# Two transformer-like blocks on one core: the order in which dense matmuls of 512 columns walk through their columns

## The chip, the core and the metric

The kernel runs on one core of one Trainium2 chip. The metric is the device time of one execution in microseconds, lower is better; a kernel is given by the median of several executions. A profile is one further execution, recorded by the hardware profiler; its span reaches from the first to the last instruction.

## The reference

One sequence of 1024 tokens of width 1024, with 16 learned tokens in front, goes through two blocks in float32. What matters here is where the dense products are:

```python
# first block
proj  = h @ w_in                       # then three mixers: HGRN2, Mamba2, S5
mixed = concatenate([y_a, y_b, y_c]) @ w_out
h  = layer_norm(ALPHA * h + mixed)
ff = square(relu(h @ w_mlp_in)) @ w_mlp_out     # 1024 -> 4096 -> 1024
h  = layer_norm(ALPHA * h + ff)
# second block: a gated delta rule and a spatial gating branch, each with its own
# projections, a gated sum, an output projection, and a feed-forward part of width 2 x 2816
```

The mixers are sequences of small products and elementwise work on chunks of tokens; the projections and the feed-forward parts are large products with K, M and N of hundreds to thousands.

## The kernel before

All tokens are processed in two halves of 512 tokens (the first with the 16 learned ones in front). Dense products keep float32 accuracy by three products of a rounded format: `split` and `weights` make of each operand a high part (ScalarE copies it to the format `F32R`, tiles `xt` and `wh`) and a low part (VectorE subtracts, tiles `xt` and `wl`). `mm3` (line 233) then adds high·high, high·low and low·high into one PSUM bank, a tile `ps` of 128 x 512 float32, of which there are four. Every matmul is issued by the helper `mm`, line 204, so nearly all TensorE rows of a profile carry that line, and the tiles tell them apart.

Two kinds of caller use `mm3`:

- `fm` (line 239) makes 128 features by up to 512 tokens: the weights are the stationary operand (`ps<-wh,xt` and `ps<-wl,xt` in the rows: the tile named first is the stationary one there) and the activations are the moving one. `unit` of the first projection, `mlp`, `p2`, `merge` and `ffn` call it.
- `out_proj` (line 1196) and `down` (line 1212) make 128 tokens by 512 features: the activations are stationary and 512 columns of the weights move (`ps<-xt,wh`, `ps<-xt,wl`, or `f` in place of `xt` where the activations lie in the mixers' tiles).

Some dense products are of other widths: 264 columns in the first projection's first half, 390 in `vd`, 344 in `sgu`. The mixers' own products call `mm` directly and write the four PSUM tiles `px`; they are in plain float32, with a few in half precision (in `delta`, line 1060 and after, where the moving operand is read in runs of 2, 4, ... 64 elements with gaps as long as the runs, `self.halves(X[:, c], 0, lb)`, and PSUM is written without gaps).

The order of the work is written by hand: `run` draws steps from generators of the dense parts and of the mixers in turns (`steps`), so that small products of a mixer stand between the large ones. On each engine the instructions run in program order.

The columns of an operand of 512 columns begin at a multiple of 16 columns of its tile (column 0, 16 or 512), and in the built program every tile begins at a multiple of 32 bytes of its partition.

Of the kernel before, what the change touches and what calls it, by code (L numbers as in the profile page):

```python
# [17 lines left out]
DRAM = bass.MemoryType.DRAM  # L18
# [6 lines left out]
ALPHA = 2.0 ** 0.25  # L25
# [4 lines left out]
# columns of the constant array  # L30
C_ID = 0
C_I10 = 128                   # 1024 times the identity
C_SGN = C_I10 + 128
C_TRI = C_SGN + 1
C_BLK = C_TRI + 128           # ones in the two diagonal 64-blocks
C_BAND = C_BLK + 128          # 64 zeros, 128 ones, 64 zeros
C_N = C_BAND + 256

# columns of the array of byte masks: the levels (only the columns in the second halves of their blocks),
# the same transposed (only the first halves), the diagonal, what is below it  # L40
# [6 lines left out]
# columns of the per-feature parameter array  # L47
P_HNW = 0
P_LB = 1
P_CW1 = P_LB + 3              # 7 x 4  # L50
# [3 lines left out]
P_GB = P_NW1 + 3  # L54
P_CWQ = P_GB + 2              # 12 x 4
P_DNW = P_CWQ + 48
P_CWF = P_DNW + 1             # 44 x 3
# [4 lines left out]
# columns of the row array (the same on all partitions)  # L62
# [7 lines left out]
# order of the feature-major tiles of the first projection  # L70
U1 = dict(u=0, f=2, q=5, g=8, xbc=11, z=18)
NU1 = 21
# ... and of the second
# [4 lines left out]
class Op:  # L78
    """The hi and lo parts of an operand."""
# [8 lines left out]
class Kb:  # L88
# [54 lines left out]
    def mask(self, o, b=None):  # L143
        """A byte mask for four blocks of 128 columns, or for the halves of a level's blocks in them."""
        n = 128
        if b is not None:
            o += 64 * LEVELS.index(b)
            n = 64
        m = self.bm[:, o:o + n].rearrange("p (o t) -> p o t", o=1).to_broadcast([128, 4, n])
        return m if b is None else m.rearrange("p c (n b) -> p c n b", b=b)  # L150

    def halves(self, x, i, b):
        """The first or second halves of the blocks of 2 b columns."""
        if len(x.shape) == 2:
            return x.rearrange("p (n s b) -> p n s b", s=2, b=b)[:, :, i, :]
        return x.rearrange("p c (n s b) -> p c n s b", s=2, b=b)[:, :, :, i, :]
# [8 lines left out]
    def t(self, w, dt=F32):  # L165
        """A working tile of the mixers."""
        return self.mx.tile([128, 528], dt, tag="f", bufs=self.NF, name=self.nm("f"))[:, :w]

    def ta(self):
        """Two working tiles of 528 columns, out of the accumulators' tiles."""  # L170
        x = self.accp.tile([128, 1056], F32, tag="acc", name=self.nm("ta"))
        return x[:, 0:528], x[:, 528:1056]
# [14 lines left out]
    # ---------------------------------------------------------------- operands  # L187
# [18 lines left out]
    def xt(self, f=False):  # L206
        """A tile for the hi and lo parts of an operand; f: out of the mixers' tiles."""
        if f:
            return Op(self.t(528, F32R), self.t(528, F32R))
        x = self.xtp.tile([128, 2, 528], F32R, tag="xt", name=self.nm("xt"))  # L210
        return Op(x[:, 0], x[:, 1])
# [4 lines left out]
    def split(self, src, w, f=False):  # L216
        """hi and lo parts of src [128, w]."""
        x = self.xt(f)
        self.act(x.hi[:, :w], src)
        self.tt(x.lo[:, :w], src, x.hi[:, :w].bitcast(F32), ALU.subtract)  # L220
        return x

    def weights(self, src, w):
        """hi and lo parts of a block of weights [128, w] in DRAM."""
        raw = self.wp.tile([128, 1032], F32, tag="wr", bufs=2, name=self.nm("wr"))
        self.nc.sync.dma_start(raw[:, :w], src)
        hi = self.wp.tile([128, 1032], F32R, tag="wh", bufs=3, name=self.nm("wh"))
        lo = self.wp.tile([128, 1032], F32R, tag="wl", bufs=3, name=self.nm("wl"))
        self.act(hi[:, :w], raw[:, :w])
        self.tt(lo[:, :w], raw[:, :w], hi[:, :w].bitcast(F32), ALU.subtract)  # L230
        return hi, lo

    def mm3(self, out, a, b, start, stop):
        """out += a^T b with hi and lo parts."""
# [4 lines left out]
    def fm(self, out, w, xs, o, n, k0=0):  # L239
        """out [128 features, n tokens] from a unit of weights and the tiles xs."""  # L240
        for k, x in enumerate(xs):
            c = 128 * (k0 + k)
# [3 lines left out]
    # ---------------------------------------------------------------- first projection  # L246
# [91 lines left out]
    # ---------------------------------------------------------------- HGRN2  # L338
    def hgrn_pre(self):
        """ln(1 - lb) and lb, a column for each pair of heads."""  # L340
# [13 lines left out]
    def hgrn(self, p, h):  # L354
# [5 lines left out]
        q = self.t(512)  # L360
# [7 lines left out]
        # log f and k  # L368
# [19 lines left out]
        # scores  # L388
# [17 lines left out]
        # the queries of a level for both heads at once, each among zeros for the other's features  # L406
# [40 lines left out]
        # decays  # L447
# [12 lines left out]
        # kd with tokens on the partitions, and what each chunk adds to the state  # L460
# [16 lines left out]
        # the states before the chunks, both heads' on the diagonal  # L477
# [20 lines left out]
        # norm and gate  # L498
# [12 lines left out]
    # ---------------------------------------------------------------- Mamba2  # L511
    def softplus(self, x, tag, w):
        """max(x, 0) + ln(1 + exp(-|x|)) in place; x is narrow."""
# [6 lines left out]
    def rows(self, x, n):  # L520
        """The sums over tokens up to each, a row in DRAM for each of the n columns of x."""
# [15 lines left out]
    def square(self, x):  # L537
        """The hi and lo parts of the square of x [128, 512]."""
# [7 lines left out]
    def sums(self, out, parts):  # L546
        """The sum of the products of ones (lhsT) and operands (p: their partitions)."""
# [4 lines left out]
    def conv4(self, src, NT, cw, cb, out):  # L552
        """Causal convolution of four taps, then silu."""
# [10 lines left out]
    def mamba(self, h):  # L564
# [8 lines left out]
        # dt and dA, with tokens on the partitions; the first six columns are the short chunk  # L573
# [19 lines left out]
        for c in range(c0, 5):  # L593
            L = 16 if c == 0 else 128
            t0 = 0 if c == 0 else R0 + 128 * (c - 1)
            # acum_t and exp(acum_t) on all partitions
# [24 lines left out]
            # x dt and B with tokens on the partitions  # L621
# [39 lines left out]
        # gate, norm  # L661
# [24 lines left out]
    # ---------------------------------------------------------------- S5  # L686
    def cmul(self, o, a, b, t):
        """o = a b for pairs (re, im) of access patterns; t: two temporaries of the shape."""
# [7 lines left out]
    def exp(self, out, x, w):  # L696
        """exp(x) to the last bits, for small tiles (w: four times the width of x)."""
# [17 lines left out]
    def s5_pre(self):  # L715
# [26 lines left out]
        # the angle, less its multiple of 2 pi  # L742
# [28 lines left out]
        # the powers of the unit phasor by doubling: 8, 16, ..., 1024 steps  # L771
# [9 lines left out]
        # input factors  # L781
# [14 lines left out]
        # mirrored powers  # L796
# [35 lines left out]
    def s5(self, qd):  # L832
        """Groups 4 qd .. 4 qd + 3, all tokens."""
# [11 lines left out]
        def outer(out, a, b, c, d, op, tmp):  # L845
            """out = a x b (op) c x d over powers and channels."""
# [25 lines left out]
        # the part within a block of 8 tokens  # L872
# [17 lines left out]
        # rotation by the angle of 8 tokens  # L890
# [59 lines left out]
    # ---------------------------------------------------------------- gated delta rule  # L950
# [7 lines left out]
    def dn_cols(self, h):  # L958
        """Columns for each chunk and head: -beta, beta, G, the rest of the chunk's decay, the whole of it."""
# [23 lines left out]
    def delta(self, hd, h, cols):  # L983
# [24 lines left out]
        # tokens on the partitions  # L1008
# [11 lines left out]
        # k k^T and k q^T with decay; N16 holds -N^T  # L1020
# [17 lines left out]
        # (I + N)^-1: a half precision inverse by doubling the diagonal blocks ...  # L1038
# [33 lines left out]
        # ... made exact by two steps Y += Y (I - (I + N)^T Y), the residual in full precision  # L1072
# [15 lines left out]
        # the chain over the chunks  # L1088
# [40 lines left out]
    # ---------------------------------------------------------------- spatial gating  # L1129
# [7 lines left out]
    def stats(self, parts, tag):  # L1137
        """Columns with the mean and 1 / sqrt(var + eps) over the free dimension of the parts."""
# [42 lines left out]
    # ---------------------------------------------------------------- the dense parts  # L1181
# [14 lines left out]
    def out_proj(self, xs, w, acc):  # L1196
        """acc = ALPHA acc + xs^T w."""
# [14 lines left out]
    def down(self, hid, w, acc, first, done=None):  # L1212
        """acc += hid^T w for a group of hidden tiles; w: [2, n / 2, 128, 1024]."""
# [17 lines left out]
    def hidden(self, make, w, acc, groups, done=None):  # L1231
        """acc += hid^T w, the hidden tiles made in groups; a group's first tile is made before the last one's product."""
# [10 lines left out]
    def ln(self, acc, gb, out=None, xs=None, f=False):  # L1243
        """Layer norm of the tiles acc in place; the hi and lo parts of its transpose into the list xs."""
# [24 lines left out]
    def ln_first(self, acc, gb, xs):  # L1269
        """The same, its transpose first: there scale and shift are columns (of the first norm)."""  # L1270
# [28 lines left out]
    def ln_last(self, acc, gb, out):  # L1299
        """Layer norm of the tiles acc, each as soon as it is complete: called for every half of one."""  # L1300
# [85 lines left out]
    def merge(self, h, ys, hs):  # L1386
        """The gated sum of the two branches' projections."""
# [47 lines left out]
    # ---------------------------------------------------------------- the whole  # L1435
# [5 lines left out]
    def seq(self, h):  # L1441
        """HGRN2 and Mamba2 of a half."""
# [11 lines left out]
    def both(self, *gs):  # L1454
        """The generators in turns."""
# [18 lines left out]
    def run(self):  # L1474
# [18 lines left out]
        # first block, first half  # L1493
# [12 lines left out]
        # second half, beside the first one's norm  # L1506
# [14 lines left out]
        # second block  # L1521
# [31 lines left out]
    def steps(self, a, n=9999, b=None, r=0.0, rest=True):  # L1553
        """Up to n steps of a, with r steps of b after each; the rest of b when a ends."""
# [25 lines left out]
def tables(nc):  # L1580
    """Loads of the activation tables, each for as many instructions as one set covers."""
# [132 lines left out]
```

## Time and profile before

| | us |
|---|---|
| median of 3 executions | 2840.01 |
| lowest and highest of them | 2832.19, 2843.59 |
| span of the profiled execution | 2831.3 |
| TensorE busy in it | 2768.6 (98%) |
| VectorE, ScalarE, GpSimd busy | 1793.7, 1163.4, 220.4 |

In the rows PE is TensorE's matmuls, PEld its weight loads, DVE VectorE, ACT ScalarE and POOL GpSimd. The "busy" of a matmul is its whole passage, some 0.39 us for 512 columns, of which the next one overlaps a part; what a matmul costs in a dense stretch is the distance from its start to the start of the next.

### The profile page before, as it was taken

The numbers are of one execution on the slowest core, as the hardware profiler recorded it, in microseconds if no ns is written. First come the engines' busy times: TensorE is split into PE (matmuls) and PEld (weight loads), VectorE is DVE, ScalarE is ACT, GpSimd is POOL, SyncE is SP. The second block draws the span as 40 slices with busy tenths as digits, with TensorE's granted clock in tenths as the row PEclk, the third lists the DMA queues.
The fourth block names the chain that finished last, engine by engine and source line by source line (L and its number), as shares of the span: only waits on it lengthen the run. The fifth ranks groups of instructions, "written<-read, shape, count | busy, mean of one in ns | idle before, by whom it ended". The sixth has DMA issues, their size and how long they took to land.

```text
span 2831.3 us, 37337 instructions
## 1 busy us (share of the span) xinstructions
PE 2768.6 (98%) x14176; PEld 2262.4 (80%) x14176; DVE 1793.7 (63%) x3321; ACT 1163.4 (41%) x1810; POOL 220.4 (8%) x365
## 2 busy tenths in 40 slices
PE   8999999999999999999999999999999999999997
PEld 7788777777878878877788888888788888888886
DVE  7678768777756554386545675535867557675556
ACT  4334344444442353364323334435545334344432
POOL 3121000000001121010000001110100000000000
PEclk9999999999999999999999999999999999999999
DMA  7333462323344444333333455433244433342232
GB/s 220 122 94 93 139 202 81 113 89 113 106 147 149 157 144 133 123 101 123 105 104 119 142 184 166 126 126 130 79 136 140 149 104 101 107 139 92 97 96 75
DMA packets 138036, 351.55 MB, mean 124 GB/s; under 512 B 26779, under 2 KB 40641, under 8 KB 137857
## 3 DMA queue, kind: packets, MB, share of 16 engines
q1 hardware_dynamic: 113712, 295.34, 32.9%
q0 software_dynamic: 16672, 48.50, 5.0%
q10 hardware_dynamic: 7473, 5.34, 0.7%
q8 instruction: 111, 1.82, 0.3%
q14 instruction: 68, 0.56, 0.1%
HBM read 296.84 MB, written 51.69 MB: 123 GB/s over the span
## 4 chain that ended last, share of the span: by engine, by line
PE 81%; issue 7%; DVE 6%; DMA 2%; ACT 2%; POOL 1%; SPq 0%; DVEq 0%; POOLq 0%; ACTq 0%
PE ps L204 73%; PE px L204 7%; DVE f L192 2%; ACT f L189 1%; DVE wl L192 1%; PE px L1265 1%; DVE f L195 1%; DMA hx<-ev 1%; DMA wr<-in_w 0%; DVE acc L195 0%; DMA f<-rows 0%; DVE f L433 0%; ACT wh L189 0%; DVE ta L192 0%; ACT ev L189 0%
## 5 line engine op out<-in xcount | busy, mean ns | idle before, releaser
L204 PE MATMUL ps<-xt,wh 128*128 128x512 f32 (+1 forms) x3616 | 1117.0, 388 | 8.7 <-ACT wh L189 8.5
L192 DVE TENSOR_TENSOR wl<-wr,wh 128x1024 fp32r<-128x1024 f32 (+3 forms) x431 | 521.5, 1210 | 606.7 <-ACT wh L189 590.2
L189 ACT ACTIVATE wh<-wr 128x1024 fp32r<-128x1024 f32 (+3 forms) x431 | 452.3, 1050 | 898.4 <-PE ps L204 826.1
L204 PE MATMUL ps<-wh,xt 128*128 128x512 f32 (+3 forms) x2624 | 813.1, 384 | 4.7 <-ACT xt L189 4.4
L204 PEld LDWEIGHTS ps<-xt,wh 128*128 128x128 f32 x3616 | 665.9, 189 | 141.7 <-ACT wh L189 8.5
L204 PE MATMUL ps<-xt,wl 128*128 128x512 f32 (+1 forms) x1808 | 698.6, 387 | 3.9 <-DVE wl L192 3.9
L204 PEld LDWEIGHTS ps<-wh,xt 128*128 128x128 f32 (+1 forms) x2624 | 485.8, 188 | 99.9 <-ACT xt L189 6.9
L204 PE MATMUL ps<-wl,xt 128*128 128x512 f32 (+3 forms) x1312 | 502.2, 383 | 0.8 <-DVE wl L192 0.7
L204 PEld LDWEIGHTS ps<-xt,wl 128*128 128x128 f32 x1808 | 341.5, 189 | 72.8 <-DVE wl L192 5.5
L204 PE MATMUL ps<-f,wh 128*128 128x512 f32 x960 | 300.5, 394 | 0.0
L204 PEld LDWEIGHTS ps<-wl,xt 128*128 128x128 f32 (+1 forms) x1312 | 246.7, 188 | 46.5 <-DVE wl L192 2.0
L189 ACT ACTIVATE f<-f 128x512 f32<-128x512 f32 (+6 forms) x300 | 178.5, 613 | 200.6 <-DVE f L192 62.3
L204 PE MATMUL px<-f,f 128*128 128x128 f32 (+8 forms) x1832 | 201.4, 258 | 16.8 <-DVE f L192 10.2
L204 PEld LDWEIGHTS ps<-f,wh 128*128 128x128 f32 x960 | 180.3, 188 | 42.3
L189 ACT ACTIVATE ev<-ps 128x512 f32<-128x512 f32 (+4 forms) x303 | 169.6, 561 | 72.9 <-PE ps L204 67.1
L192 DVE TENSOR_TENSOR acc<-acc,ps 128x512 f32<-128x512 f32 x192 | 130.8, 683 | 95.8 <-PE ps L204 93.9
L204 PE MATMUL ps<-f,wl 128*128 128x512 f32 x480 | 189.4, 394 | 0.0
L204 PEld LDWEIGHTS px<-f,f 128*128 128x128 f32 (+2 forms) x1192 | 133.3, 180 | 52.9 <-issue 22.8
L192 DVE TENSOR_TENSOR f<-f,f 128x256 f32<-128x256 f32 (+5 forms) x244 | 128.6, 547 | 39.0 <-ACT f L189 37.0
L189 ACT ACTIVATE xt<-ev 128x512 fp32r<-128x512 f32 x131 | 82.3, 629 | 149.2 <-DVE ev L192 145.9
L195 DVE SCALAR_TENSOR_TENSOR ev<-ev,p,ev 128x512 f32<-128x512 f32 x176 | 132.2, 751 | 2.7 <-ACT ev L189 0.6
L192 DVE TENSOR_TENSOR xt<-ev,xt 128x512 fp32r<-128x512 f32 x124 | 85.9, 696 | 49.6 <-ACT xt L189 49.1
(223 smaller groups left out, 2046.9 us busy)
## 6 DMA issues: line engine op xcount, KB each, us to landing
wr<-in_w SPq DMA_DIRECT2D x93, 512.0 KB, 3.8
wr<-in_wup SPq DMA_DIRECT2D x88, 512.0 KB, 3.5
wr<-in_wmi SPq DMA_DIRECT2D x64, 512.0 KB, 3.6
wr<-in_wmo SPq DMA_DIRECT2D x64, 512.0 KB, 3.6
wr<-in_wdn SPq DMA_DIRECT2D x44, 512.0 KB, 3.5
wr<-in_wo SPq DMA_DIRECT2D x32, 512.0 KB, 3.7
Y<-f POOLq DMA_DIRECT2D x32, 256.0 KB, 2.6
ev<-Y SPq DMA_DIRECT2D x32, 256.0 KB, 3.6
```

The source lines that it names most:

```text
L189: self.nc.scalar.activation(out=out, in_=in_, func=func, **kw)
L192: self.nc.vector.tensor_tensor(out=out, in0=a, in1=b, op=op)
L195: self.nc.vector.scalar_tensor_tensor(out=out, in0=a, scalar=s, in1=b, op0=op0, op1=op1)
L204: self.nc.tensor.matmul(out, lhsT, rhs, start=start, stop=stop)
L1265: nc.tensor.transpose(b[:, 128 * t:128 * t + 128], acc[t][:, 128 * k:128 * k + 128], self.ident)
```

## The change

In `mm3`, where the output has 512 columns, the output and both moving operands are given as patterns of three dimensions: column 16 a + 4 b + e is visited with b as the outer count (4), a in the middle (32) and e inside (4). So the columns come in the order 0-3, 16-19, 32-35, ... 496-499, then 4-7, 20-23, and so on. Output and moving operand go in the same order, so every column lands where it did before. The stationary operand, the other widths, the mixers' products and all other engines' instructions stay.

```diff
     def mm3(self, out, a, b, start, stop):
+        if out.shape[-1] == 512:
+            order = lambda y: y.rearrange("p (a b e) -> p b a e", a=32, e=4)
+            out, b = order(out), [order(y) for y in b]
         self.mm(out, a[0], b[0], start, False)
         self.mm(out, a[0], b[1], False, False)
         self.mm(out, a[1], b[0], False, stop)
```

The rest of the diff takes out comments. In the built program 9648 matmuls have the new pattern, the number of 512-column matmuls into `ps`. No instruction changes its place on any engine. What differs beside the shape is a few waits of TensorE on its own semaphore (`PE_49`): 229 in the program before, 330 now, since the dependencies between writes of different patterns into one bank are found differently.

On TensorE, in the first projection of the second half of tokens (a unit's bank `ps_1425`, with the hgrn mixer's small products `px` around it), before:

```order
L204 MATMUL px_1391<-f_1257,f_1384 128x128 x3
L204 MATMUL ps_1425<-xt_103,wh_1420 128x512 x2
L204 MATMUL ps_1425<-xt_103,wl_1421 128x512
L204 MATMUL ps_1425<-xt_108,wh_1420 128x512 x2
L204 MATMUL ps_1425<-xt_108,wl_1421 128x512
```

and now:

```order
L204 MATMUL px_1391<-f_1257,f_1384 128x128 x3
L204 MATMUL ps_1425<-xt_103,wh_1420 128x4x32x4 [waits PE_49]
L204 MATMUL ps_1425<-xt_103,wh_1420 128x4x32x4
L204 MATMUL ps_1425<-xt_103,wl_1421 128x4x32x4
L204 MATMUL ps_1425<-xt_108,wh_1420 128x4x32x4 x2
L204 MATMUL ps_1425<-xt_108,wl_1421 128x4x32x4
```

Nothing moved: the shape is another one, and the first matmul into the bank waits for an earlier matmul of TensorE's own. In these listings the moving tile stands first.

## Rows read from the trace of the kernel before

**Rows 1.** The page, part 1: busy us and share of each engine.

```profile
PE 2768.6 (98%) x14176; PEld 2262.4 (80%) x14176; DVE 1793.7 (63%) x3321; ACT 1163.4 (41%) x1810; POOL 220.4 (8%) x365
```

**Rows 2.** The page, part 4: chain that ended last, by engine and by line.

```profile
PE 81%; issue 7%; DVE 6%; DMA 2%; ACT 2%; POOL 1%; SPq 0%; DVEq 0%; POOLq 0%; ACTq 0%
PE ps L204 73%; PE px L204 7%; DVE f L192 2%; ACT f L189 1%; DVE wl L192 1%; PE px L1265 1%; DVE f L195 1%; DMA hx<-ev 1%; DMA wr<-in_w 0%; DVE acc L195 0%; DMA f<-rows 0%; DVE f L433 0%; ACT wh L189 0%; DVE ta L192 0%; ACT ev L189 0%
```

**Rows 3.** TensorE groups, shapes apart: xcount | busy us, mean ns | idle before.

```profile
L204 PE MATMUL ps<-xt,wh 128*128 128x512 f32 x3232 | 1042.0, 399 | 0.2 <-ACT xt L189 0.2
L204 PE MATMUL ps<-wh,xt 128*128 128x512 f32 x2096 | 679.1, 398 | 4.7 <-ACT xt L189 4.4 <-DVE acc L195 0.3
L204 PE MATMUL ps<-xt,wl 128*128 128x512 f32 x1616 | 643.2, 398 | 2.6 <-DVE wl L192 2.6
L204 PE MATMUL ps<-wl,xt 128*128 128x512 f32 x1048 | 416.0, 397 | 0.2 <-DVE wl L192 0.2
L204 PE MATMUL ps<-f,wh 128*128 128x512 f32 x960 | 300.5, 394 | 0.0
L204 PE MATMUL ps<-f,wl 128*128 128x512 f32 x480 | 189.4, 394 | 0.0
...
L204 PE MATMUL ps<-wh,f 128*128 128x512 f32 x144 | 47.0, 395 | 0.0
...
L204 PE MATMUL ps<-wl,f 128*128 128x512 f32 x72 | 28.3, 394 | 0.0
L1265 PE MATMUL px<-c,acc 128*128 128x128 f32 x160 | 21.0, 272 | 0.0
```

**Rows 4.** TensorE's waits, longest: us in total, times, longest.

```profile
PE px L204 <- DVE f L192: 11.4, 12, 2.8
PE ps L204 <- ACT wh L189: 8.5, 1, 8.5
```

**Rows 5.** Timeline of TensorE, full clock: start us, us, instruction, xcount.

```profile
999.77 0.39 PE L204 MATMUL ps<-xt,wh 128*128 128x512 f32 x1
1000.00 0.40 PE L204 MATMUL ps<-xt,wl 128*128 128x512 f32 x1
1000.23 0.62 PE L204 MATMUL ps<-xt,wh 128*128 128x512 f32 x2
1000.70 0.39 PE L204 MATMUL ps<-xt,wl 128*128 128x512 f32 x1
...
1005.79 0.40 PE L204 MATMUL ps<-xt,wh 128*128 128x512 f32 x1
```

**Rows 6.** Stretches: us, PE, PEld, DVE, ACT, POOL busy (x), PEclk, DMA share, GB/s.

```profile
1000.00:1006.00 6.00, 6.00 (x27) 4.88 (x26) 1.23 (x1) 1.54 (x2) 1.07 (x2) 1.00 0.37 122
2033.40:2036.60 3.20, 3.17 (x15) 2.27 (x16) 2.71 (x7) 0.00 (x0) 0.00 (x0) 0.50 0.49 164
```

**Rows 7.** Timeline of TensorE in the stretch at half clock.

```profile
2034.42 1.05 PE L204 MATMUL ps<-wh,xt 128*128 128x512 f32 x2
2035.28 0.63 PE L204 MATMUL ps<-wl,xt 128*128 128x512 f32 x1
2035.70 1.05 PE L204 MATMUL ps<-wh,xt 128*128 128x512 f32 x2
2036.56 0.37 PE L204 MATMUL px<-f,f 128*128 128x64 f16 x4
```

**Rows 8.** Timeline, half precision: runs of 2 (twice), then without gaps.

```profile
1068.90 0.29 PE L204 MATMUL px<-f,f 128*128 128x64 f16 x4
1069.03 0.41 PE L204 MATMUL ps<-wh,xt 128*128 128x344 f32 x1
...
1265.88 0.29 PE L204 MATMUL px<-f,f 128*128 128x64 f16 x4
1266.01 0.48 PE L204 MATMUL ps<-xt,wh 128*128 128x512 f32 x1
...
1115.73 0.29 PE L204 MATMUL px<-f,f 128*128 128x64 f16 x4
1115.86 0.71 PE L204 MATMUL ps<-xt,wh 128*128 128x512 f32 x2
```

## Prediction

> **What bounds the kernel now.** I read the busy times first: TensorE's matmuls cover 98% of the span, VectorE 63%, ScalarE 41% [rows 1]. The chain of work that ended last agrees: 73% of the span is matmuls into the `ps` banks [rows 2]. The waits say that little is left beside them: the longest group of TensorE's waits is 11.4 us in all, the next 8.5 us [rows 4]. So a nanosecond on a dense matmul is a nanosecond on the end, and the question is what one such matmul costs and how many there are.
>
> How many: the eight groups into `ps` with 512 columns have 3232 + 2096 + 1616 + 1048 + 960 + 480 + 144 + 72 = 9648 matmuls [rows 3], all of those that the change rewrites. What one costs is not the mean of 394 to 399 ns in these rows, which overlaps with the next, but the distance between starts. From 999.77 to 1005.79 us stand 26 of them back to back [rows 5] (three in each of eight repeats, one before and one after), at a granted clock of 1.00 [rows 6]: 6.02 / 26 = 231.5 ns. 9648 x 231.5 ns = 2234 us, 79% of the span of 2831.3 us. One nanosecond more or less on each is 9.65 us, 0.34% of the time. A measurement of this kernel can tell about 0.5% from no change, 14 us, or 1.5 ns a matmul.
>
> **What these 231.5 ns consist of.** [...] If everything in a matmul went with TensorE's clock, it would cost 214 ns at full clock; it costs 17.5 ns more. [...] That 17.5 ns, 169 us over all 9648, is the only thing in these rows that an order of columns can give back. [...]
>
> **The change part by part.**
>
> The work in the array is the same: 512 columns, the same products, the same weight loads. Cost nothing; the 214 ns stay.
>
> The moving operand is read in 128 runs of four columns, each run elsewhere than the last, where it was one run of 512. No row before has a float32 read of this kind. The nearest are the half precision products of the gated delta rule. In its first round their moving operand has 32 runs of two elements with gaps; four of them take 1068.90 to 1069.03 us, and in another place 1265.88 to 1266.01; in the last round, with one run of 64, four take 1115.73 to 1115.86 [rows 8]. All are 0.13 us, 32.5 ns each. So 31 jumps cost nothing that can be seen. The starts are given to 10 ns; a difference of 10 ns over 4 x 31 jumps would be 0.08 ns a jump. 127 jumps are then at most 10.2 ns a matmul, 99 us in all. From below the bound is the 17.5 ns: -169 us. I take zero: what is seen in the nearest row is no cost, though that row moves half as many bytes a column, and so is not at the edge of its supply. That is the weak point of the argument, and both ends stay for the range.
>
> PSUM is written in the same order, 128 runs of four columns. No matmul before writes PSUM with gaps, and no row is near. Between the bounds of a gain of 17.5 ns and a loss to the rate at half clock (428 - 231.5 = 196.5 ns a matmul, below) I take zero, since the half precision rows, the nearest there are, show that a pattern of several dimensions as such costs nothing to step through, and since in the new order each run still holds four neighbouring columns, which is the same number of neighbours that any grouping by two or four would see before.
>
> [...]
>
> The waits: 101 more waits of TensorE on its own semaphore stand in the program, nearly all on the first matmul into a `ps` bank and for a matmul at least 17 places back. TensorE runs in order, and there is no row in which it waits for itself; the 160 transposes of line 1265, some of which carry such a wait, have 0.0 us of idle time before them [rows 3]. I take zero. If each instead let the matmul before it run out (0.39 us of passage less the 0.23 between starts [rows 5], so 0.16 us), 145 first matmuls would cost 23 us. The wait is for work long done, so I don't add it to the range's end. Behind a waiting matmul stand all later ones, and behind them ScalarE and VectorE, which have 59% and 37% of their time free [rows 1].
>
> The sum is 0 us: 2831.3 us for a span like the one profiled, and 2840 us against the median of the three executions, 2840.01, which lies 8.7 us above that span.
>
> **The rivals.**
>
> *A better order.* Reading neighbouring places one after the other may be what costs the 17.5 ns, when neighbours lie in one part of the memory that is not ready again in time; an order that jumps 64 bytes each time would then spread them. For it: the surcharge is there at full clock and gone at half, so it is a matter of supply. Against: nothing shows that it depends on the order. All of it back gives 2840 - 9648 x 17.5 ns = 2671 us, half of it 2756. After that TensorE would still be the bound, as VectorE's 1794 us and ScalarE's 1163 us are far below [rows 1].
>
> *A poorer order, little.* Jumps cost up to 0.08 ns each, the finest that the half precision rows can hide. 2840 to 2939 us. It decides from 1.5 ns a matmul, 0.012 ns a jump.
>
> *A poorer order, much.* The 17.5 ns may be a cost of each block of sixteen columns (64 bytes): 17.5 / 32 = 0.55 ns. In the new order each run of four is in another block than the one before, 128 visits where there were 32: 96 x 0.55 = 52.5 ns more, 9648 times, 506 us: 3346 us. It counts from the first jump, and nothing hides it. For it: the surcharge exists and the block of sixteen is a size at which it could arise. Against: the half precision rows, where the jumps are free.
>
> *PSUM.* Every column written costs what it does at half clock: 231.5 goes to 428 ns, +1896 us: 4736 us. Against it: the runs of four. [...]
>
> That the change doesn't do what it says can be left out: in the built program the shape 128x4x32x4 stands on 9648 matmuls.
>
> **How the numbers follow.** No change within 0.5%: 0.37. A better order: 0.30, with anything from 14 to 169 us. A poorer one by a little: 0.17; by much: 0.12; PSUM: 0.04. So faster 0.30, same 0.37, slower 0.33. The likeliest single case gives 2840 us. The first three cases lie between 2671 and 2939 us and hold 0.84, so the range is 2670 to 2940; it leaves out 0.16. The likeliest case alone would be 2826 to 2854.
>
> **What would show it.** In the profile after, the distance between starts in a dense stretch like that of rows 5: 231.5 ns by the forecast, 214 ns by the better order, 242 ns at the end of the little loss, 284 ns by the cost of a block, 428 ns by PSUM. If the same distance at half clock stays at 428 ns while that at full clock changes, it is supply; if both change, it is PSUM or the stepping itself. TensorE waiting for itself would appear among the waits. The forecast is wrong if the supply of the moving operand, which half precision never brings to its edge, answers to the order.

## The result and the profile after

| | before | after |
|---|---|---|
| median of 4 executions | 2841.8 | 2798.38 us |
| lowest and highest | 2832.19, 2843.59 | 2794.46, 2800.17 us |
| span of the profiled execution | 2831.3 | 2798.3 us |

Before has one execution more than in the table ahead of the prediction.

The ratio after to before is 0.986, with a 95% interval of 0.9845 to 0.9875. The change makes the kernel faster by 1.4%, 40 us; the two medians stand 43 us apart. The forecast was no change, 2840 us, with 2670 to 2940 as the range: the range holds the time, the likeliest case did not come, and the rival "a better order" came with about a quarter of the 169 us that it could give.

The page after, parts 1 and 4, beside [rows 1, 2]:

```profile
PE 2722.5 (97%) x14176; PEld 2261.6 (81%) x14176; DVE 1793.5 (64%) x3321; ACT 1162.4 (42%) x1810; POOL 220.4 (8%) x365
...
PE 76%; issue 8%; DVE 8%; DMA 4%; ACT 3%; POOL 1%; SPq 0%; DVEq 0%; POOLq 0%; ACTq 0%
```

The instruction counts and the work of VectorE, ScalarE and GpSimd are those of before. Only the matmuls' time fell, by 46 us.

What one matmul costs is best read where nothing else is in the way. Near the end of the program, in the last feed-forward part, stands an unbroken stretch of 512-column matmuls that begins and ends at the same instructions in both kernels. Of the stretch in time the row gives the length in us, then busy time and count of PE, PEld, DVE and ACT, the granted clock, the busy share of the DMA engines and GB/s. The busy times are here those of the instructions on `ps` alone. First the kernel before, then the one after:

```profile
2412.89:2799.15 386.26, 386.26 (x1666) 312.40 (x1664) 36.26 (x54) 26.71 (x46) 1.00 0.31 103
```

```profile
2390.02:2766.21 376.19, 376.19 (x1666) 311.99 (x1664) 36.30 (x54) 26.76 (x46) 1.00 0.33 105
```

The window runs from the start of the first to the start of the last matmul. Two of the 1666 are not a distance of their own (the last, and the one whose passage still reaches in), so 1664 distances: 386.26 / 1664 = 232.1 ns before, 376.19 / 1664 = 226.1 ns after. That is 6.0 ns less, at a granted clock of 1.00 in both. Over all places in the trace where one 512-column matmul on `ps` follows another within 300 ns (8958 and 8949 places), the means are 231.7 and 226.2 ns, 5.5 ns less; 9648 x 5.5 ns = 53 us.

At half clock nothing changed. The row that answers to [rows 6] and the rows that answer to [rows 7], after:

```profile
2016.00:2022.70 6.70, 6.16 (x35) 4.72 (x36) 3.70 (x8) 1.72 (x3) 0.00 (x0) 0.50 0.54 151
```

```profile
2018.33 1.05 PE L204 MATMUL ps<-wh,xt 128*128 128x512 f32 x2
2019.18 0.63 PE L204 MATMUL ps<-wl,xt 128*128 128x512 f32 x1
2019.61 1.05 PE L204 MATMUL ps<-wh,xt 128*128 128x512 f32 x2
2020.47 0.44 PE L204 MATMUL px<-f,f 128*128 128x64 f16 x4
```

Five matmuls from 2018.33 to 2020.47 us are 428 ns each, at a granted clock of 0.50, as the five of [rows 7] are. The prediction's 214 ns are half of that: an estimate of what a matmul takes at full clock if all of it goes with the clock, called the array's below. The 17.5 ns are what its 231.5 ns have beyond them. So the gain, 6.0 ns at full clock and none at half, is taken from what shows at full clock only, as the prediction's test for "supply" asked.

The 53 us of shorter matmuls did not all arrive. In the two profiled executions TensorE's busy time fell by 46.1 us, the rest of the span grew from 62.7 to 75.8 us, and so the span is only 33.0 us shorter. (The medians differ by more, 43 us, since the profiled execution before is some 10 us shorter than the median of its kernel.) TensorE now waits more for others. Its longest waits, beside [rows 4]:

```profile
PE px L204 <- DVE f L192: 13.8, 12, 3.2
PE px L204 <- ACT f L189: 9.5, 13, 1.6
PE ps L204 <- ACT wh L189: 9.1, 2, 8.7
PE ps L204 <- DVE wl L192: 7.6, 7, 4.2
```

The first was 11.4 us before. All idle time of TensorE that a wait ended went from 48 to 60 us. There is no wait of TensorE for itself among the waits, though 330 such waits stand in the program. Between the 53 us of the count and the 46 us of busy time stands the granted clock, with a mean of 0.992 in the trace before and 0.990 after: some 5 us, by an estimate from these two numbers.

### The profile page after: what moved, and what is told of

Its sections match the earlier page's. It is cut to its first block, busy times and chain, and to the rows that moved or that the text cites. A ratio compares the mean times of both kernels' runs of the same rounds, so it can differ in the third digit from the quotient of the medians.

```text
span 2798.3 us, 37325 instructions
## 1 busy us (share of the span) xinstructions
PE 2722.5 (97%) x14176; PEld 2261.6 (81%) x14176; DVE 1793.5 (64%) x3321; ACT 1162.4 (42%) x1810; POOL 220.4 (8%) x365
## 4 chain that ended last, share of the span: by engine, by line
PE 76%; issue 8%; DVE 8%; DMA 4%; ACT 3%; POOL 1%; SPq 0%; DVEq 0%; POOLq 0%; ACTq 0%
PE ps L204 68%; PE px L204 7%; DVE f L192 2%; ACT f L189 2%; DVE wl L192 1%; DVE ta L192 1%; DVE f L195 1%; DMA ev<-gt 1%; PE px L1268 1%; DMA f<-rows 1%; DVE acc L195 1%; DMA wr<-in_w 1%; DMA cx<-qkv 1%; ACT wh L189 1%; DMA f<-in_xT 0%
## 5 line engine op out<-in xcount | busy, mean ns | idle before, releaser
L204 PE MATMUL ps<-xt,wh 128*128 128x512 f32 (+1 forms) x3616 | 1098.3, 382 | 8.9 <-ACT wh L189 8.7
L204 PE MATMUL ps<-wh,xt 128*128 128x512 f32 (+3 forms) x2624 | 804.3, 380 | 8.2 <-ACT xt L189 4.9
L204 PE MATMUL ps<-xt,wl 128*128 128x512 f32 (+1 forms) x1808 | 683.9, 378 | 6.6 <-DVE wl L192 6.6
L204 PE MATMUL ps<-f,wh 128*128 128x512 f32 x960 | 293.5, 386 | 0.0
```

Source lines behind the costliest of these rows:

```text
L204: self.nc.tensor.matmul(out, lhsT, rhs, start=start, stop=stop)
```

## The experiments

Each kernel is the one before or after with the lines shown. The distance between starts is that of the stretch above in each kernel's own trace; the times are medians against the kernel before on the same chip. In the table "step" is how far the runs stand from each other.

| order of the columns | distance, ns | time, us | ratio (interval) |
|---|---|---|---|
| straight on (before) | 232.1 | 2841.8 beside the change, 2835.64 to 2838.7 beside the others | 1 |
| runs of 4, step 8 (32 bytes) | 232.1 | 2838.93 | 1.0005 (0.9995 to 1.0016) |
| runs of 4, step 16 (64 bytes), the change | 226.1 | 2798.38 | 0.986 (0.9845 to 0.9875) |
| runs of 4, step 32 (128 bytes) | 244.9 | 2944.17 | 1.0379 (1.036 to 1.0399) |
| runs of 4, step 64 (256 bytes) | 278.0 | 3243.13 | 1.1424 (1.1405 to 1.1444) |
| runs of 4, step 128 (512 bytes) | 267.6 | 3145.77 | 1.1085 (1.1068 to 1.1103) |
| runs of 2, step 16 | 434.9 | 4741.05 | 1.6706 (1.668 to 1.6732) |
| runs of 8, step 16 | 232.1 | 2838.84 | 1.0011 (0.9997 to 1.0025) |
| runs of 16, step 64 | 238.4 | 2889.57 | 1.0184 (1.0162 to 1.0205) |
| only the reads as in the change | 226.1 | 2798.02 | 0.9862 (0.9843 to 0.9882) |
| only the writes as in the change | 232.1 | 2839.66 | 1.0003 (0.999 to 1.0017) |
| only the writes, runs of 2, step 16 | 232.1 | 2836.57 | 1.0003 (0.9992 to 1.0013) |
| straight on, weights from one column | 232.5 | 2844.46 | 1.0017 (1.0008 to 1.0027) |
| the change, weights from one column | 224.9 | 2788.77 | 0.9821 (0.9805 to 0.9837) |

### Which side: reads or writes

My theory after the result was that the moving operand's supply answers to the order of its reads; the rival was that PSUM's writes do. The change in `mm3` was cut in two:

```diff
-            out, b = order(out), [order(y) for y in b]
+            b = [order(y) for y in b]
```

> Only the moving operand is read by fours sixteen columns apart; PSUM is written straight on, so the columns of every dense result come out in another order. In the changed kernel the distance between starts of 512-column matmuls fell from 231.6 to 226.2 ns in the mean. If the gain is on the side of the reads, this kernel keeps it: 226 ns and about 2798 us. If it is on the side of PSUM, it loses it: 231.6 ns and about 2841 us. If one side gains and the other loses, it is below 226 ns and below 2798 us.

```diff
-            out, b = order(out), [order(y) for y in b]
+            out = order(out)
```

> Only PSUM is written by fours sixteen columns apart; the moving operand is read straight on, so the columns of every dense result come out in another order. Reads: 231.6 ns and about 2841 us, as before. PSUM: 226 ns and 2798 us. If writes with gaps cost something that the reads pay for, above 232 ns and above 2850 us.

The stretch with the reads alone, then with the writes alone:

```profile
2391.16:2767.35 376.19, 376.19 (x1666) 312.26 (x1664) 36.27 (x54) 26.74 (x46) 1.00 0.34 105
```

```profile
2421.83:2808.09 386.26, 386.26 (x1666) 312.66 (x1664) 36.30 (x54) 26.70 (x46) 1.00 0.33 103
```

376.19 us is to the hundredth what the changed kernel takes, 386.26 us what the one before takes. The reads carry the whole gain, and the writes cost nothing that shows and bring nothing. Since runs of four leave every pair of neighbours together, one more kernel wrote PSUM by pairs:

```diff
-            order = lambda y: y.rearrange("p (a b e) -> p b a e", a=32, e=4)
-            out, b = order(out), [order(y) for y in b]
+            order = lambda y: y.rearrange("p (a b e) -> p b a e", a=32, e=2)
+            out = order(out)
```

> Only PSUM is written by runs of two columns, 16 columns apart; the moving operand is read straight on, and the columns of the dense results come out in another order. Runs of four cost nothing on this side (e2_psum_only, 231.7 ns). If PSUM asks for pairs, this costs nothing either: 231.7 ns, 2840 us. If it asks for more neighbours than two, it is slower.

```profile
2416.60:2802.86 386.26, 386.26 (x1666) 312.69 (x1664) 36.32 (x54) 26.67 (x46) 1.00 0.32 103
```

386.26 us again, 232.1 ns a matmul: writes by pairs cost nothing that shows either. A pace of the writes that is quicker than that of the reads would stay hidden: for runs of four anything up to the 226.1 ns of the changed kernel, for runs of two anything up to 232.1 ns.

The two kernels with gaps in the writes have ratios of 1.0003 each, so for runs of four and of two columns, 64 bytes apart, gaps in the writes cost nothing that shows. Writes of single columns were not tried.

### Is it the meeting with the weight loads?

Why a read straight on costs 17.5 ns more than the array, the prediction told only as a possibility, under the rival "a better order". Another possibility is that the moving operand's reads meet those of the weight load that runs beside every matmul [rows 1]. To take the weight load's walk through memory away, its columns were all read from one place, in the kernel before and in the changed one:

```diff
+        if out.shape[-1] == 512:
+            a = [y[:, 0:1].to_broadcast([128, 128]) for y in a]
```

> The kernel before, with the moving operand and PSUM straight on, but every dense matmul of 512 columns loads its stationary operand from one column, repeated 128 times: a weight load then touches one place of memory and not 128 columns in a row, and the dense results are wrong. If the 17.5 ns that a matmul costs beyond the array's own 214 ns come from reads of the weight load that meet those of the moving operand, most of it goes: 214 to 218 ns between starts, 2671 to 2710 us. If the moving operand is held up by itself, by the order of its own reads alone, nothing changes: 231.6 ns and 2840 us.

> As e5_one_column, with the moving operand and PSUM by fours sixteen columns apart. If the order matters only through meetings with the weight load, this kernel is as fast as e5_one_column (214 to 218 ns). If it matters by itself, it is 5.4 ns a matmul faster than e5_one_column, as the changed kernel is against the one before, and stands at 226 ns where e5_one_column stands at 231.6.

```profile
2425.80:2812.62 386.82, 386.82 (x1666) 313.98 (x1664) 36.37 (x54) 26.67 (x46) 1.00 0.32 102
```

```profile
2381.86:2756.09 374.23, 374.23 (x1666) 311.99 (x1664) 36.13 (x54) 26.77 (x46) 1.00 0.33 106
```

In both kernels the second of the two cases came, in the latter 1.1 ns below the 226 named. Straight on, 386.82 / 1664 = 232.5 ns: the surcharge stays whole, so it is not made by where the weight load reads. That the weight load reads at all beside each matmul was not taken away (PEld is busy for 313.98 us, before for 312.40). With the change, 374.23 / 1664 = 224.9 ns, 1.2 ns below the changed kernel: in the new order a small part depends on the weight load's walk after all. The difference between the two orders, 7.6 ns here, is there without it. So the order of the reads counts by itself.

The traffic of the other engines is another rival, and the trace before answers it. In the stretch, the distance is 232.3 ns in the mean where VectorE, ScalarE or GpSimd work over 90% of the time (1210 distances) and 232.6 ns where none of them works (218); it is 231.8 ns with the DMA engines over 40% busy (560) and 232.1 ns with less than 2% (855). So the surcharge does not follow their traffic.

### Which step, which run

The remaining kernels changed the order's two sizes, on both sides, so that the results stay in place. The writes alone were measured only for runs of four and of two with the step of 64 bytes; that the other orders' cost is the reads' is argued from there, not shown. The expectations call four columns in a row, 16 bytes, a line. First the step, with runs of four:

```diff
-            order = lambda y: y.rearrange("p (a b e) -> p b a e", a=32, e=4)
+            order = lambda y: y.rearrange("p (a b e) -> p b a e", a=64, e=4)   # a=16, a=8, a=4
```

> Runs of four, 8 columns (32 bytes) apart, on both sides. Measured so far in distances between starts: straight on 231.6 ns, 16 columns apart 226.2, 32 apart 245.2, and runs of sixteen 64 apart 238.4. If lines 64 bytes apart are the one good step, this lies near 231.6 ns (2840 us). If what counts is how the reads run against those of the weight load, which go straight on through 512 bytes, every order has a number of its own, and this one lies anywhere between 214 and 250 ns.

> Runs of four, 32 columns (128 bytes) apart instead of 16, on both sides. If the gain is that neighbouring lines are not read one after the other, the distance between them does not matter: 226 ns, 2798 us. If it is a structure of 64 bytes that the sixteen columns just fit, the gain is another one, and at 128 bytes may grow (towards 214 ns, 2671 us) or be lost (231.6 ns, 2841 us).

> Runs of four, 64 columns (256 bytes) apart, on both sides. If a larger step than 64 bytes stays in one part of the memory for longer, as the 245.2 ns at 128 bytes would have it, this is slower still: 250 ns or more, over 2990 us. If the step of 128 bytes is a case of its own, this is between 226 and 238 ns.

> Runs of four, 128 columns (512 bytes) apart, on both sides. So far: 8 apart 232.0 ns between starts, 16 apart 226.2, 32 apart 245.2, 64 apart 280.2, straight on 231.7. If the reads are spread over four parts of 64 bytes each that repeat every 256 bytes, a step of 256 bytes or any multiple always meets the same part, and 512 bytes cost what 256 do: 280 ns, about 3243 us. If the parts repeat at a larger distance, each doubling of the step adds about twice as much as the one before: 345 ns or so, over 3800 us.

The stretch, in that order:

```profile
2423.17:2809.38 386.21, 386.21 (x1666) 312.78 (x1664) 36.36 (x54) 26.71 (x46) 1.00 0.32 103
```

```profile
2505.81:2931.49 425.68, 425.68 (x1740) 331.58 (x1738) 41.06 (x61) 26.73 (x46) 1.00 0.30 94
```

```profile
2741.18:3224.37 483.19, 483.19 (x1740) 334.77 (x1738) 41.10 (x61) 27.69 (x46) 1.00 0.26 83
```

```profile
2664.63:3129.64 465.01, 465.01 (x1740) 334.79 (x1738) 41.11 (x61) 27.43 (x46) 1.00 0.27 86
```

(In the last three the unbroken stretch runs on to TensorE's last matmul, 74 more, so 1738 distances.) The time is not a matter of how many jumps there are, nor of the pattern having three dimensions: these orders and the change have the same 128 runs of four columns, and lie between 226 and 278 ns. It is how far each jump goes. The expectations came for 32 and 256 bytes. For 128 bytes none of the three distances that I named (226, 214, 231.6 ns) came, and for 512 bytes the nearer of the two cases, 280 ns and 3243 us, was 12 ns and 97 us too high.

Per step, as the excess over the array's 214 ns divided by the number of such steps (the jumps back between two passes left out): 64 bytes (16 columns), 124 steps, 12.1 ns, 0.10 ns; 128 bytes, 120 steps, 30.9 ns, 0.26 ns; 256 bytes, 112 steps, 64.0 ns, 0.57 ns; 512 bytes, 96 steps, 53.6 ns, 0.56 ns. From 256 to 512 bytes a step costs no more. The four parts of 64 bytes, in one case of the expectation for 512 bytes, are not shown by that. With the jumps back that stay in one such part (124 and 120 steps in all) the last two are 0.52 and 0.45 ns, not the same; and straight on, 96 of the 127 steps from one 16 bytes to the next stay in the same 64 bytes, and cost only 18.1 / 96 = 0.19 ns each.

At half clock the step of 512 bytes is not felt either. It takes 267.6 ns at full clock; at a granted clock of 0.50 five matmuls take 428 ns each, from 2232.14 to 2234.28 us:

```profile
2232.14 1.05 PE L204 MATMUL ps<-wh,xt 128*128 128x512 f32 x2
2232.99 0.63 PE L204 MATMUL ps<-wl,xt 128*128 128x512 f32 x1
2233.42 1.05 PE L204 MATMUL ps<-wh,xt 128*128 128x512 f32 x2
2234.28 0.33 PE L204 MATMUL px<-f,f 128*128 128x64 f16 x2
```

Then the runs: twice as long, half as long, and sixteen columns as one block:

```diff
-            order = lambda y: y.rearrange("p (a b e) -> p b a e", a=32, e=4)
+            order = lambda y: y.rearrange("p (a b e) -> p b a e", a=32, e=8)   # a=32, e=2;  a=8, e=16
```

> Runs of eight columns (two lines of 16 bytes), 16 columns apart, on both sides. If the gain comes from leaving a block of 64 bytes after each line, two lines in a row lose half of it: 229 ns, about 2820 us. If it comes from the step of 64 bytes as such, whatever is read there, it stays: 226 ns, 2798 us. If it takes a single line in each block, it is gone: 231 to 232 ns, 2840 us, as with lines 32 bytes apart, which also meet each block twice.

> Runs of two columns (half a line of 16 bytes), 16 columns apart, on both sides: each line is visited twice, with 32 visits to others between. If a visit to a line has a price of its own that four columns just hide, 256 visits and not 128 show it: well above 231.7 ns. If only the step of 64 bytes counts, 226 ns and 2798 us. Writes by pairs alone are in e12_psum_pairs, to be taken off.

> Runs of sixteen columns (64 bytes), 64 columns apart, on both sides: within a run the lines are read straight on, only blocks of 64 bytes are taken out of order. If neighbouring 16-byte lines read one after the other are the cost, three of four steps are still such: a quarter of the gain, 230 ns, 2830 us. If the cost arises between blocks of 64 bytes, all of the gain is here: 226 ns, 2798 us.

The stretch with runs of eight, of two and of sixteen:

```profile
2415.07:2801.25 386.18, 386.18 (x1666) 314.01 (x1664) 36.37 (x54) 26.65 (x46) 1.00 0.33 103
```

```profile
4079.67:4725.56 645.89, 645.89 (x1487) 305.48 (x1485) 32.26 (x47) 23.61 (x41) 1.00 0.17 53
```

```profile
2460.12:2857.10 396.98, 396.98 (x1667) 314.81 (x1665) 36.33 (x54) 26.75 (x46) 1.00 0.32 100
```

(The stretch of the runs of two begins 253 matmuls later and runs to the last, 1485 distances; that of the runs of sixteen has 1665.) Runs of eight lose the whole gain: 232.1 ns, as straight on and as step 8, which also visit a block of 64 bytes more than once in a row. Of the orders tried, only one gained: a single run of four, 16 bytes, in each block, and then the next block. Sixteen at a time, 256 bytes apart, are slower than straight on by 6.3 ns; my expectation there (230 or 226 ns) missed on both sides.

Runs of two show a price of a visit. 645.89 / 1485 = 434.9 ns for 256 visits is 1.70 ns a visit of two columns; 226.1 / 128 = 1.77 ns is a visit of four in the changed kernel, and 232.1 / 64 = 3.63 ns one of eight. In the array four columns take 214 / 128 = 1.67 ns (an estimate). So a visit of two columns costs about what one of four does, and a run of two pays it twice as often. (The writes are in pairs there too, which by themselves left 232.1 ns.) It does not go with TensorE's clock, as the stretch at half clock of the same kernel shows:

```profile
3285.00:3288.00 3.00, 3.00 (x14) 1.93 (x11) 2.36 (x6) 0.00 (x0) 0.00 (x0) 0.50 0.56 195
```

```profile
3285.56 1.07 PE L204 MATMUL ps<-wh,xt 128*128 128x512 f32 x2
3286.46 0.61 PE L204 MATMUL ps<-wl,xt 128*128 128x512 f32 x1
3286.89 1.04 PE L204 MATMUL ps<-wh,xt 128*128 128x512 f32 x2
3287.76 0.41 PE L204 MATMUL px<-f,f 128*128 128x64 f16 x4
```

3285.56 to 3287.76 us are five matmuls of 440 ns, at half clock hardly slower than at full; a price that went with the clock would have doubled. This agrees with a surcharge that shows at full clock only: there 128 visits of 1.70 ns are 217.5 ns (an estimate) beside the array's 214; at half clock 128 visits of 440 / 256 = 1.72 ns are 220 ns (an estimate) beside 428, and runs of four are not felt in the two orders read there, 428 ns with steps of 64 and of 512 bytes.

## Why the prediction was right and wrong

- **What bounds the kernel**: right. A dense matmul's nanosecond is the kernel's: 9648 x 5.5 ns = 53 us, of which 40 to 43 arrived. In the slow orders it holds the same way: step 32 is 12.8 ns a matmul, 123 us by the count, 107 us measured.
- **The 17.5 ns as a limit of supply, gone at half clock**: the reason that the range reached down to 2671 us. No run shows a matmul of 214 ns at full clock, so none shows the 17.5 ns as a whole; the 214 are an estimate, half of the 428 ns at a granted clock of 0.50 [rows 6, 7], and the shortest distance that a run showed is 224.9 ns. A supply at its edge, of which the zero below speaks, no run shows either. Right as far as the runs go: the change gives back 5.5 ns at full clock, the reads alone do it, and the distance at half clock stays at 428 ns.
- **The moving operand's new order at zero**: this is the step that failed, as a term of the wrong size. It measured -5.5 ns over all places (-6.0 in the stretch) and was taken as zero from the half precision rows [rows 8]. Those rows could not have shown it: 5.5 ns over 127 jumps is 0.043 ns a jump, and by the prediction's own count they tell nothing below 0.08. And they are another case. Their runs of two elements lie 8 bytes apart, so that every second jump stays within 16 bytes and each 16 bytes still give four columns. The prediction named its weak point, that half precision moves half the bytes a column, and still took the value.
- **The range**: it held partly by luck. Its upper end, from 10.2 ns a matmul for 127 jumps, counts jumps and not how far they go. It would have been the same for runs of four with steps of 128, 256 and 512 bytes, which measured 2944, 3243 and 3146 us (+12.8, +45.9 and +35.5 ns), all beyond 2940.
- **PSUM at zero**: right for the change, by a kernel of its own; runs of two cost nothing that shows either. The reason given, the half precision rows, was no evidence on writes with gaps: those rows write without gaps.
- **The waits of TensorE on itself at zero**: right as far as it shows: there is none among its waits. The kernel with the new pattern on the writes alone has as many of these waits in its trace as the changed kernel, 330, where the kernel before and the one with the reads alone have 229; and its time is 1.0003 of before.
- **What comes late next**: not costed. I wrote that TensorE would stay the bound, which is so, but in the profiled executions TensorE's waits for VectorE and ScalarE, whose work stayed the same, grew by some 12 us.
- **The rivals**: "a better order" came, with about a third of its 17.5 ns. Its mechanism, that neighbouring places read one after the other cost something and a jump of 64 bytes spreads them, agrees with the 232.1 ns of the orders that visit 64 bytes more than once in a row, but does not tell why larger jumps are slower, and is not shown. "A poorer order, little" did not come. "Much poorer, by the block of sixteen" was wrong for this order, though one with a larger step is nearly as bad as it feared (278.0 ns against 284), for another reason, since the number of visits is the same. "PSUM" fell: the writes alone leave 232.1 ns, where it has 428.

What stays open: why the order of the reads matters, and why even the best order keeps 12 ns over the array's 214. The 1.2 ns that went with the weight load's walk are a part of these 12; 3.5 are what 128 visits at 1.70 ns take beyond the array (an estimate).

## What to carry to other kernels

Where a matmul's start-to-start distance at full clock is more than half of that at half clock, something that does not go with the clock is in it. Here, at 231.7 ns beside 428, that was at least in part the reads of the moving operand, and their order is then worth a try: runs of 16 bytes, 64 bytes apart, gave 1.4%, while steps of 128, 256 and 512 bytes cost 4 to 14%, and runs of 8 bytes 67%. A price for an access pattern is to be taken from rows with the same bytes per column and the same steps, and fine enough to show it; the half precision rows were neither. PSUM took runs of four and of two, 64 bytes apart, at no cost that shows.

## What was not expected of the hardware

- The order of the columns has a price that depends on the step and not on the number of jumps: 226.1, 244.9 and 278.0 ns a matmul for steps of 64, 128 and 256 bytes, then 267.6 for 512.
- Reading straight on is not the best order: 232.1 ns, as runs of four 32 bytes apart (232.1) and runs of eight 64 bytes apart (232.1), where runs of four 64 bytes apart take 226.1.
- A run of two float32 columns costs about as much as one of four with the same step: 434.9 ns for 256 visits against 226.1 ns for 128, and 440 ns for the 256 at half clock.
- PSUM writes with gaps, in runs of four and of two columns 64 bytes apart, cost nothing that shows: ratios of 1.0003 (0.999 to 1.0017) and 1.0003 (0.9992 to 1.0013).
